# Moving columns of the projections' matrix products read in groups of 16, last group first

## The chip, the cores and the metric

The kernel runs on one NeuronCore of a Trainium2 chip. The metric is the device time of one execution in microseconds (us). Three runs of the kernel before gave 1861.96, 1864.28 and 1864.6 us; the median, 1864.28 us, is the time that the change is measured against.

## The reference, cut to what matters

Two layers of a hybrid block work on an activation of 512 positions by 1024 features. Each layer is a chain of matrix products with small element-wise pieces between them:

```python
h = rms_norm(x, g_pre_mix)
proj = h @ w_in                          # 1024 -> 6728 columns: q, k, v, qi, ki, wi, xr, gr, zu, zv, gates
y_a = dsa_attention(q, k, v, qi, ki, wi) # 8 heads, top-128 keys by an indexer
y_b = rg_lru(conv(xr)) * gelu(gr)
y_c = chunked_spatial_gating(gelu(zu), rms_norm(gelu(zv)), w_spatial, b_spatial)
branch = einsum('nbsw,nwd->nbsd', stack(y_a, y_b, y_c), w_branch)
merged = einsum('bsnd,nbsd->bsd', sigmoid(gates), branch)
x = x + rms_norm(merged @ w_out, g_post_mix)
f = square(relu(rms_norm(x, g_pre_ffn) @ w_ffn_up)) @ w_ffn_down   # 1024 -> 4096 -> 1024
x = x + rms_norm(f, g_post_ffn)
x = x + rms_norm((p_i @ w_ple) * sigmoid(x @ w_ple_gate), g_post_ple)
```

## The kernel before, in words

**Layout.** Activations lie transposed: features on the 128 partitions, the 512 positions along the free dimension, eight tiles of 128x512 for 1024 features. So most products take a 128x128 block of weights as the stationary operand and a 128x512 activation tile as the moving one, and sum eight such products (one for each tile of features) in one 2 KB bank of PSUM, 128 partitions by 512 columns of 4 bytes.

**Three products for one.** Each operand is held as a sum of a high and a low part of the type float32r (`split`, line 365, for activations; `prep`, line 231, for weights). A product of two such operands is three matmuls into the same bank: high by high, low weights by high activations, high weights by low activations. The helper `mm3` (line 296, its matmuls on lines 297, 298 and 299) issues these three; `gemm` (line 301) calls it for each tile of features.

**The callers.** `gemm` serves the input projections (`proj`, line 555), the branch products (`branch`, line 870), the output projection (line 1036), the feed-forward products (lines 1062 and 1071), the two products of the last stage (lines 1103 and 1122) and, in halves of 256 columns, the last three tiles of the output projection and of the last gate (`gemm_halves`, line 321). `mm3` is also called by itself for the spatial gating (line 765, moving operands of 256 columns) and for the gates of the recurrence (lines 829 and 830). `gemm_arriving` (line 334, matmul on line 355) starts the first outputs of a stage while their activation tiles are still being made, tile by tile, in whole tiles of 512 columns or in two halves of 256; `ordered` (line 311) writes the order of its instructions down by hand. `tokens` (line 578, matmul on line 589) computes the two projections whose result is wanted with positions on the partitions: there the activations are the stationary operand, and the weights, 512 columns wide, the moving one.

**What is not reached by the change.** The indexer's and the attention's products (lines 655, 658 and 941), the transposes (lines 162, 433, 630 and 927), the sums of squares (line 407) and the 120 small matmuls at the start (line 113) call the engine directly.

**What feeds and follows.** Weights arrive by SyncE's queue in 128x1024 blocks (line 236); ScalarE makes the high part (line 242) and VectorE the low part (line 243), three blocks ahead (`getw`, line 246). Eight banks of PSUM are used in turn; VectorE or ScalarE reads a bank once its last matmul is done. Waits between engines are put in by the framework from the tiles and regions that the instructions read and write; each engine works through its own instructions in the order of the program. Work of the indexer, attention and recurrence is dealt out between matmuls by a clock that counts estimated matmul time (`tick`, line 285).

Of the kernel before, what the change touches and what calls it, by code (L numbers as in the profile page):

```python
# [19 lines left out]
KT = 8  # L20
# [30 lines left out]
def hybrid_block_kernel(ctx, tc, xT, pT, pos, vec, bsp, freq, w_in, w_tok, w_lru, w_sp, w_br, w_out, w_up, w_dn, w_ple, w_gate, out, depth=DEPTH, dbg=None):  # L51
    nc = tc.nc
    V, A, G, PE = nc.vector, nc.scalar, nc.gpsimd, nc.tensor
# [13 lines left out]
    def tmp(dt=F32):  # L67
        return tp.tile([128, S], dt, tag="tmp", name=nm("tmp"), bufs=NTMP)
# [4 lines left out]
    def bank():  # L73
        return pp.tile([128, 512], F32, tag="ps", name=nm("ps"), bufs=8)

    def slot(tag, dt=F32, big=False):
        return cp.tile([128, 4, S] if big else [128, S], dt, tag=tag, name=nm(tag))
# [5 lines left out]
    def width(r):  # L83
        return r.stop - r.start
# [146 lines left out]
    def prep():  # L231
        i = nprep[0]
        nprep[0] += 1
        key, src = order[i]
        raw = wp.tile([128, 1024], F32, tag="wr", name=nm("wr"), bufs=3)
        nc.sync.dma_start(raw, src)
        if key[0] == "sp":
            r3 = raw.rearrange("p (g t) -> p g t", g=8)
            G.affine_select(out=r3, in_=r3, compare_op=ALU.is_ge, fill=0.0, base=0, pattern=[[0, 8], [1, 128]], channel_multiplier=-1)
        hi = wp.tile([128, 1024], F32R, tag="wh", name=nm("wh"), bufs=NWB)  # L240
        lo = wp.tile([128, 1024], F32R, tag="wl", name=nm("wl"), bufs=NWB)
        A.copy(hi, raw)  # L242
        V.tensor_sub(lo, raw, f32v(hi))  # L243
        prepared[key] = (hi, lo)

    def getw(key, ahead=LA):
        assert order[nget[0]][0] == key, (order[nget[0]][0], key)
        nget[0] += 1
        while nprep[0] < min(nget[0] + ahead, len(order)):
            prep()  # L250
        return prepared.pop(key)
# [33 lines left out]
    def tick(us):  # L285
        clk[0] += us
        run_later()
        run_tasks()
# [4 lines left out]
            tick(0.3)  # L293


    def mm3(ps, wh, wl, xh, xl, start, stop):
        PE.matmul(ps, wh, xh, start=start, stop=False)  # L297
        PE.matmul(ps, wl, xh, start=False, stop=False)  # L298
        PE.matmul(ps, wh, xl, start=False, stop=stop)  # L299

    def gemm(ps, w, xs, kk, c0=0, st=None, r=FULL):

        h3, l3 = [v.rearrange("p (k c) -> p k c", k=kk) for v in w]
        for k in range(kk):
            if st is not None and k == kk - 2:
                st.partial()
            mm3(ps, h3[:, k, c0:c0 + 128], l3[:, k, c0:c0 + 128], xs[k][0][:, r], xs[k][1][:, r], k == 0, k == kk - 1)
            tick(0.65 * width(r) / S)

    @contextmanager  # L310
    def ordered(last):

        cur = nc.cur_bb
        n0 = len(cur.bb.instructions)
        yield
        for i in cur.bb.instructions[n0:]:
            if i.engine in last:
                tc.add_manual_dep(i, last[i.engine], mybir.DependencyInfo(mybir.DependencyClass.NoSync, mybir.DependencyReason.DATA), reason="ordered")
            last[i.engine] = i.name
# [14 lines left out]
    def gemm_arriving(keys, xs, source, ranges, arrived=None, lag=LAG, tail=TAIL):  # L334


        n = len(keys)
        ws = [getw(key, 0) for key in keys[:-1]]
        pss = [bank() for _ in keys]
        last = {}  # L340
        for r in ranges:
            gen = source(r)
            for k in range(KT):
                with ordered(last):
                    next(gen)
                    todo = [(o, k) for o in range(len(ws))]
                    if len(ws) < n and k == lag:
                        ws.append(getw(keys[-1], 0))
                        todo += [(n - 1, q) for q in range(k + 1)]
                    if r is ranges[-1] and k >= KT - tail:  # L350
                        todo = [] if k < KT - 1 else [(o, q) for o in range(n) for q in range(KT - tail, KT)]
                    for i, (o, q) in enumerate(todo):
                        h3, l3 = [v.rearrange("p (k c) -> p k c", k=KT) for v in ws[o]]
                        for m in range(3):
                            PE.matmul(pss[o][:, r], (h3, l3, h3)[m][:, q], xs[q][m // 2][:, r], start=q == 0 and m == 0, stop=q == KT - 1 and m == 2)  # L355
                        if r is ranges[-1] and q == KT - 1 and o < n - 1:
                            prep()
                tick(0.65 * len(todo) * width(r) / S)
            if arrived is not None:
                arrived(r)  # L360
        while nprep[0] < nget[0] + LA:
            prep()
        return pss
# [84 lines left out]
    class Norm:  # L448
# [16 lines left out]
        def source(self, r):  # L465
            while r.start not in self.gens:
                tick(0.1)
            return self.gens[r.start]
# [48 lines left out]
    for k in range(KT):  # L517
        if k in FIRST:
            c = slice(128 * k, 128 * (FIRST + [KT])[FIRST.index(k) + 1])
# [12 lines left out]
    for l in range(depth):  # L532
# [22 lines left out]
        def proj(name, ahead=LA):  # L555
            ps = bank()
            gemm(ps, getw(("in", l, name), ahead), XS, KT)
            return ps
# [19 lines left out]
        def tokens(n, fn):  # L578


            ws = [[v.rearrange("p (k c) -> p k c", k=2) for v in getw(("tok", l, n, c), LA if c == 0 else 0)] for c in range(4)]
            for t0 in (0, 2):
                pss = [bank(), bank()]
                for k in range(KT):
                    wh, wl = [v[:, k % 2] for v in ws[k // 2]]
                    for t, ps in enumerate(pss, t0):
                        xh, xl = [v[:, t * 128:(t + 1) * 128] for v in XS[k]]
                        for i, (x, w) in enumerate(((xh, wh), (xl, wh), (xh, wl))):
                            PE.matmul(ps, x, w, start=k == 0 and i == 0, stop=k == KT - 1 and i == 2)  # L589
                        tick(0.65)  # L590
                    if t0 == 2 and k in (1, 3, 5):
                        prep()
                for t, ps in enumerate(pss, t0):
                    fn(t, ps)
# [7 lines left out]
        for j in range(4):  # L602
            ps = first[j]
# [7 lines left out]
            xh, xl = slot(f"B{j}", F32R), slot(f"B{4 + j}", F32R)  # L611
# [5 lines left out]
        ps = proj("ki")  # L617
# [28 lines left out]
        for j in range(4):  # L646
            ps = proj(f"qi{j}")
# [90 lines left out]
        for j in range(4):  # L738
            ps = proj(f"zu{j}")
# [16 lines left out]
        for j in range(4):  # L756
            mx = tmp()
            m3 = mx.rearrange("p (c t) -> p c t", c=4)
            fs = slice(j * 128, (j + 1) * 128)
            for hf in range(2):  # L760
                ps = bank()
                p3 = ps.rearrange("p (c t) -> p c t", c=2)
                for c in range(2):
                    cc = 2 * hf + c
                    mm3(p3[:, c], zvh[:, cc, fs], zvl[:, cc, fs], wsh[:, j], wsl[:, j], True, True)
                for s in range(2):
                    r = slice(64 * s, 64 * s + 64)
                    V.scalar_tensor_tensor(m3[r, 2 * hf:2 * hf + 2], p3[r, :, s * 128:(s + 1) * 128], vc[r, V_GV + j:V_GV + j + 1],
                                           bs3[r, j, None, :].to_broadcast([64, 2, 128]), op0=ALU.mult, op1=ALU.add)
            G.tensor_mul(mx, mx, gzu[:, j])  # L770
            MX.append(mx)
            tick(1.3)
            tick(1.3)
            if j % 2 == 1:
                gelu_gate(j // 2, LA if j == 3 else LA - 1)
# [47 lines left out]
        for j in range(4):  # L823
            if j == 2:

                th0 = gate(2, 0, ahead=LA - 1)
            xc, xh, xl = XC[j]
            pr, pi = bank(), bank()
            mm3(pr, w3[0][:, j], w3[1][:, j], xh, xl, True, True)
            mm3(pi, w3[0][:, 4 + j], w3[1][:, 4 + j], xh, xl, True, True)  # L830
            r, i = tmp(), tmp()
            A.activation(r, pr, AF.Sigmoid, bias=col(V_BA + j))
            A.activation(i, pi, AF.Sigmoid, bias=col(V_BX + j))
            G.tensor_mul(xc, xc, i)
            Rg.append(r)
            tick(1.3)
# [160 lines left out]
        for j in range(4):  # L997
            f = rope(proj(f"q{j}"))
            q2, ql = (slot(f"A{j}", F32R), slot(f"A{4 + j}", F32R)), tmp(F32R)
            for s in range(2):  # L1000
                r, other = slice(64 * s, 64 * s + 64), slice(64 - 64 * s, 128 - 64 * s)
# [15 lines left out]
        for d in range(8):  # L1017
            if d % 2 == 0:
                w = getw(("br", l, 0, d // 2))
# [14 lines left out]
        for d in range(5):  # L1034
            ps = bank()
# [8 lines left out]
        ps = bank()  # L1044
# [52 lines left out]
        for c in range(2):  # L1097
            w = getw(("ple", l, c), ahead=1)
            if c == 1:
                bc = st3.rstd_bc()  # L1100
            for i in range(4):
                ps = bank()
# [14 lines left out]
        for d in range(5):  # L1117
            if d < 4:
                ps = first[d]
            else:  # L1120
                ps = bank()
# [95 lines left out]
```

## Time and profile before

| | |
|---|---|
| median of three runs | 1864.28 us (1861.96 to 1864.6) |
| the profiled execution's own time | 1858.77 us |
| its span, first to last instruction | 1857.0 us |
| busy TensorE matmuls (PE) | 1812.3 us, 8798 matmuls |
| busy weight loads (PEld) | 1502.8 us, 8798 loads |
| busy VectorE (DVE) / ScalarE (ACT) / GpSimd (POOL) | 1158.3 / 801.9 / 365.0 us |
| mean granted clock of TensorE | 0.993 |
| moved from and to HBM | 164.19 and 2.10 MB, 90 GB/s over the span |

The profile is one execution. Matmuls overlap one another, and the ends that the profile gives them are modelled: a 512-column matmul has a row of 0.39 us while the next one starts 0.23 us after it. What a matmul costs in a dense stretch is therefore read from the starts of neighbours, and not from the duration of a row. Weight loads run beside matmuls and have rows of their own. [...]

### The profile page before, as it was taken

The numbers are of one execution on the slowest core, as the hardware profiler recorded it, in microseconds if no ns is written. First come the engines' busy times: TensorE is split into PE (matmuls) and PEld (weight loads), VectorE is DVE, ScalarE is ACT, GpSimd is POOL, SyncE is SP. The second block draws the span as 40 slices with busy tenths as digits, with TensorE's granted clock in tenths as the row PEclk, the third lists the DMA queues.
The fourth block names the chain that finished last, engine by engine and source line by source line (L and its number), as shares of the span: only waits on it lengthen the run. The fifth ranks groups of instructions, "written<-read, shape, count | busy, mean of one in ns | idle before, by whom it ended". The sixth has DMA issues, their size and how long they took to land.

```text
span 1857.0 us, 22869 instructions
## 1 busy us (share of the span) xinstructions
PE 1812.3 (98%) x8798; PEld 1502.8 (81%) x8798; DVE 1158.3 (62%) x1939; ACT 801.9 (43%) x1292; POOL 365.0 (20%) x292
## 2 busy tenths in 40 slices
PE   8999999999999999999999999999999999999997
PEld 7778777788888888888886887887888888888886
DVE  7689976666386253533686999666563852535355
ACT  5456436564453222223454572465544432222233
POOL 3513222210240000003454141222003200000033
PEclk9999999999999999999999999999999999999999
DMA  5122222222223322232212222222222223232321
GB/s 172 63 91 89 91 94 91 68 80 80 84 88 103 102 93 101 96 109 91 92 58 96 69 91 94 99 80 69 91 80 91 91 91 102 91 102 93 112 80 58
DMA packets 49679, 167.77 MB, mean 90 GB/s; under 512 B 6049, under 2 KB 8865, under 8 KB 49569
## 3 DMA queue, kind: packets, MB, share of 16 engines
q1 hardware_dynamic: 47376, 163.64, 26.5%
q10 hardware_dynamic: 2192, 2.67, 0.4%
q8 instruction: 69, 1.13, 0.3%
q14 instruction: 42, 0.34, 0.1%
HBM read 164.19 MB, written 2.10 MB: 90 GB/s over the span
## 4 chain that ended last, share of the span: by engine, by line
PE 73%; DVE 12%; POOL 6%; issue 4%; ACT 4%; DMA 0%; SPq 0%; POOLq 0%; ACTq 0%; DVEq 0%
PE ps L297 21%; PE ps L299 20%; PE ps L298 20%; PE ps L355 3%; PE ps L589 3%; DVE tmp L693 2%; DVE wl L243 2%; DVE m L691 2%; POOL tmp L574 1%; POOL tmp L575 1%; PE ps L941 1%; PE ps L658 1%; POOL sacc L397 1%; POOL X L482 1%; PE ps L655 1%
## 5 line engine op out<-in xcount | busy, mean ns | idle before, releaser
L242 ACT CAST wh<-wr 128x1024 fp32r<-128x1024 f32 x303 | 317.1, 1049 | 459.7 <-PE ps L299 381.4
L243 DVE TENSOR_TENSOR wl<-wr,wh 128x1024 fp32r<-128x1024 f32 x303 | 386.4, 1278 | 197.0 <-ACT wh L242 196.9
L297 PE MATMUL ps<-xh,wh 128*128 128x512 f32 (+1 forms) x1296 | 504.8, 389 | 0.0
L298 PE MATMUL ps<-xh,wl 128*128 128x512 f32 (+1 forms) x1296 | 495.0, 382 | 1.2 <-DVE wl L243 1.2
L299 PE MATMUL ps<-xl,wh 128*128 128x512 f32 (+1 forms) x1296 | 495.1, 382 | 0.0
L397 POOL TENSOR_TENSOR sacc<-sacc,tmp 128x256 f32<-128x256 f32 (+1 forms) x99 | 109.8, 1109 | 894.8 <-issue 584.5
L297 PEld LDWEIGHTS ps<-xh,wh 128*128 128x128 f32 x1296 | 243.7, 188 | 49.0 <-issue 4.9
L299 PEld LDWEIGHTS ps<-xl,wh 128*128 128x128 f32 x1296 | 243.7, 188 | 48.3
L298 PEld LDWEIGHTS ps<-xh,wl 128*128 128x128 f32 x1296 | 244.1, 188 | 44.4 <-DVE wl L243 2.0
L299 PE MATMUL ps<-V,wh 128*128 128x512 f32 (+1 forms) x528 | 195.4, 370 | 0.0
L297 PE MATMUL ps<-K,wh 128*128 128x512 f32 (+1 forms) x432 | 158.2, 366 | 0.0
L298 PE MATMUL ps<-K,wl 128*128 128x512 f32 (+1 forms) x432 | 157.8, 365 | 0.0
L299 PE MATMUL ps<-B,wh 128*128 128x512 f32 x336 | 130.9, 390 | 0.0
L297 PE MATMUL ps<-A,wh 128*128 128x512 f32 x320 | 125.0, 390 | 0.0
L298 PE MATMUL ps<-A,wl 128*128 128x512 f32 x320 | 124.5, 389 | 0.0
L1076 DVE TENSOR_TENSOR M<-M,ps 128x512 f32<-128x512 f32 x48 | 33.0, 688 | 141.4 <-PE ps L299 141.4
L299 PEld LDWEIGHTS ps<-V,wh 128*128 128x128 f32 x528 | 99.5, 188 | 16.8
L1064 DVE TENSOR_TENSOR tmp<-ps,R 128x512 f32<-128x512 f32 x64 | 43.8, 689 | 108.6 <-PE ps L299 108.6
L355 PE MATMUL ps<-xl,wh 128*128 128x256 f32 (+1 forms) x264 | 87.9, 333 | 7.8 <-DVE xl L502 7.1
L298 PEld LDWEIGHTS ps<-K,wl 128*128 128x128 f32 x432 | 81.5, 189 | 13.1
L297 PEld LDWEIGHTS ps<-K,wh 128*128 128x128 f32 x432 | 81.5, 189 | 13.1
L355 PE MATMUL ps<-xh,wh 128*128 128x256 f32 (+1 forms) x264 | 86.2, 327 | 1.2 <-ACT xh L492 1.2
(239 smaller groups left out, 2742.6 us busy)
## 6 DMA issues: line engine op xcount, KB each, us to landing
wr<-in_w_in_dram SPq DMA_DIRECT2D x95, 512.0 KB, 3.3
wr<-in_w_up_dram SPq DMA_DIRECT2D x64, 512.0 KB, 3.3
wr<-in_w_dn_dram SPq DMA_DIRECT2D x64, 512.0 KB, 3.3
wr<-in_w_br_dram SPq DMA_DIRECT2D x24, 512.0 KB, 3.2
wr<-in_w_tok_dram SPq DMA_DIRECT2D x16, 512.0 KB, 3.2
wr<-in_w_out_dram SPq DMA_DIRECT2D x16, 512.0 KB, 3.2
wr<-in_w_gate_dram SPq DMA_DIRECT2D x16, 512.0 KB, 3.2
X<-in_xT_dram SPq DMA_DIRECT2D x8, 256.0 KB, 5.7
```

Of the source, the lines that this page charges most:

```text
L242: A.copy(hi, raw)
L243: V.tensor_sub(lo, raw, f32v(hi))
L297: PE.matmul(ps, wh, xh, start=start, stop=False)
L298: PE.matmul(ps, wl, xh, start=False, stop=False)
L299: PE.matmul(ps, wh, xl, start=False, stop=stop)
L355: PE.matmul(pss[o][:, r], (h3, l3, h3)[m][:, q], xs[q][m // 2][:, r], start=q == 0 and m == 0, stop=q == KT - 1 and m == 2)
L397: G.tensor_add(sacc[:, r], sacc[:, r], self.q[r.start, r.stop])
L589: PE.matmul(ps, x, w, start=k == 0 and i == 0, stop=k == KT - 1 and i == 2)
L691: V.max(m8, (sc if r == 0 else wk)[:, :n])
L693: V.match_replace(wk[:, :n], m8, (sc if r == 0 else wk)[:, :n], -3.0e38)
L1064: V.tensor_mul(t, ps, R)
L1076: V.tensor_add(F[d], F[d], ps)
```

## The change

A helper `back` takes a view of a tile whose last dimension is a multiple of 16 columns, sees it as groups of 16, and runs over the groups from the last to the first; the columns of a group stay in ascending order. A helper `mm` issues a matmul whose moving operand and whose output are both seen through `back`, so every column's sum lands where it landed before. The stationary operand is left as it is. `mm3`, `gemm_arriving` and `tokens` issue their matmuls through `mm`. The number of instructions, their order, their operands and their tiles are the same.

```diff
+    def back(v):
+
+        return v.rearrange("p (b c) -> p b c", c=16)[:, ::-1]
+
+    def mm(ps, w, x, start, stop):
+
+        PE.matmul(back(ps), w, back(x), start=start, stop=stop)
+
     def mm3(ps, wh, wl, xh, xl, start, stop):
-        PE.matmul(ps, wh, xh, start=start, stop=False)
-        PE.matmul(ps, wl, xh, start=False, stop=False)
-        PE.matmul(ps, wh, xl, start=False, stop=stop)
+        mm(ps, wh, xh, start, False)
+        mm(ps, wl, xh, False, False)
+        mm(ps, wh, xl, False, stop)
@@ gemm_arriving
-                            PE.matmul(pss[o][:, r], (h3, l3, h3)[m][:, q], xs[q][m // 2][:, r], start=q == 0 and m == 0, stop=q == KT - 1 and m == 2)
+                            mm(pss[o][:, r], (h3, l3, h3)[m][:, q], xs[q][m // 2][:, r], q == 0 and m == 0, q == KT - 1 and m == 2)
@@ tokens
-                            PE.matmul(ps, x, w, start=k == 0 and i == 0, stop=k == KT - 1 and i == 2)
+                            mm(ps, x, w, k == 0 and i == 0, k == KT - 1 and i == 2)
```

## Rows read from the trace of the kernel before

**Rows 1.** The page: busy time by engine, and the chain that ended last, by engine.

```profile
PE 1812.3 (98%) x8798; PEld 1502.8 (81%) x8798; DVE 1158.3 (62%) x1939; ACT 801.9 (43%) x1292; POOL 365.0 (20%) x292
...
PE 73%; DVE 12%; POOL 6%; issue 4%; ACT 4%; DMA 0%; SPq 0%; POOLq 0%; ACTq 0%; DVEq 0%
```

**Rows 2.** One stretch of the feed-forward stage: columns as named in the first line.

```profile
core 0: us, PE busy (x) PEld busy (x) DVE busy (x) ACT busy (x) POOL busy (x), PEclk, DMA share, GB/s
...
600.00:750.00 150.00, 150.00 (x663) 124.24 (x662) 62.51 (x72) 40.82 (x48) 0.00 (x0) 1.00 0.28 95
```

**Rows 3.** Timeline of PE, feed-forward, 512 columns: start, duration; first and sixteenth matmul.

```profile
600.44 0.39 PE L297 MATMUL ps<-xh,wh 128*128 128x512 f32 x1
...
603.84 0.39 PE L297 MATMUL ps<-xh,wh 128*128 128x512 f32 x1
```

**Rows 4.** Timeline of PE in `gemm_arriving`, 256 columns: first and twenty-first matmul.

```profile
535.55 0.28 PE L355 MATMUL ps<-xh,wh 128*128 128x256 f32 x1
...
537.95 0.28 PE L355 MATMUL ps<-xl,wh 128*128 128x256 f32 x1
```

**Rows 5.** Whole span, one line's instructions alone: lines 297, 298, 299, 355, 589, in turn.

```profile
0.00:1857.00 1857.00, 867.25 (x2256) 424.44 (x2256) 0.99 0.27 90
...
0.00:1857.00 1857.00, 855.24 (x2256) 424.84 (x2256) 0.99 0.27 90
...
0.00:1857.00 1857.00, 855.43 (x2256) 424.35 (x2256) 0.99 0.27 90
...
0.00:1857.00 1857.00, 135.65 (x792) 117.31 (x792) 0.99 0.27 90
...
0.00:1857.00 1857.00, 96.92 (x384) 74.06 (x384) 0.99 0.27 90
```

**Rows 6.** Groups of PE by shape: 256-column matmuls of lines 297 and 355.

```profile
L355 PE MATMUL ps<-xh,wh 128*128 128x256 f32 x176 | 51.2, 291 | 0.0
...
L297 PE MATMUL ps<-xh,wh 128*128 128x256 f32 x96 | 27.5, 286 | 0.0
L297 PE MATMUL ps<-K,wh 128*128 128x256 f32 x96 | 27.5, 286 | 0.0
...
L297 PE MATMUL ps<-wh,K 128*128 128x256 f32 x32 | 9.0, 282 | 0.0
```

**Rows 7.** Timeline of PE in the first stage: first and sixth of six neighbours.

```profile
23.60 0.63 PE L355 MATMUL ps<-xh,wh 128*128 128x512 f32 x1
...
25.73 0.63 PE L355 MATMUL ps<-xl,wh 128*128 128x512 f32 x1
```

**Rows 8.** The stretch around them, columns as in Rows 2.

```profile
23.50:26.00 2.50, 2.50 (x7) 1.92 (x7) 2.39 (x8) 0.00 (x0) 0.00 (x0) 0.50 0.02 7
```

**Rows 9.** Lines 433 and 927: weight loads of one column repeated, and of 128 columns.

```profile
L433 PEld LDWEIGHTS ps<-ident,rt x40: 132/134/179, 38.1 to 1848.5; 128*128 128x128 f32 x40
...
L927 PEld LDWEIGHTS ps<-ident,tmp x160: 138/141/144, 291.8 to 1356.9; 128*128 128x128 f32 x160
```

**Rows 10.** Lines 372 and 481 on VectorE, min/median/max ns: four separate groups of 64 columns, one run of 256.

```profile
L372 DVE SCALAR_TENSOR_TENSOR V<-ps,rt,V x16: 467/476/484, 245.2 to 1176.6; 128x256 fp32r<-128x256 f32 x16
...
L481 DVE SCALAR_TENSOR_TENSOR B<-B,gp,ps x32: 468/472/480, 922.7 to 1853.0; 128x256 f32<-128x256 f32 x32
```

**Rows 11.** PE's waits for other engines: in total, times, longest us.

```profile
PE ps L355 <- DVE xl L502: 7.1, 9, 3.8
PE ps L655 <- DVE A L642: 6.7, 10, 1.2
PE ps L589 <- DVE wl L243: 5.0, 2, 2.5
```

## The prediction

> **What bounds the kernel now.** I read the page first: busy times, then the chain that ended last [rows 1]. Matmuls fill 1812.3 of 1857.0 us, so TensorE is without work for 44.7 us in all, and 73% of the chain is its own. A busy row of overlapping matmuls says little of their pace, so next I took a dense stretch [rows 2]: 150 us in the feed-forward stage without a gap, granted clock 1.00 (the 2.4 GHz level), VectorE and ScalarE busy for 62.5 and 40.8 us of it, the DMA engines for 0.28. Nothing but TensorE can set the time there. Then the pace, from neighbours' starts. Fifteen steps of 512-column matmuls take 3.40 us [rows 3], 226.7 ns each. Twenty steps of 256 columns take 2.40 us [rows 4], 120.0 ns each. The difference, 106.7 ns for 256 columns, is 0.417 ns a column, one column per clock at 2.4 GHz; what is left is the same in both, 13.3 to 13.4 ns per matmul. So a matmul costs its columns plus a fixed part, and there is no slack that would swallow a slower column: the moving read and the write of the sums run as fast as the array takes them.
>
> PE's waits for other engines are few [rows 11]; the longest total is 7.1 us. A slower TensorE could win back a part of the 44.7 us and no more.
>
> **The change, part by part.** No instruction is added, removed or moved. No queue is passed, no DMA touched, no buffer changed, no wait added by intention. What changes is the address pattern of two operands of 2256 matmuls on each of lines 297, 298 and 299, 792 on line 355 and 384 on line 589 [rows 5]: 7944 of 8798.
>
> - *How many are narrow.* On line 297, 96 + 96 + 32 = 224 have 256 columns, and lines 298 and 299 have as many; on line 355 it is 176 for each of three products [rows 6]. Together 3 x 224 + 3 x 176 = 1200. The other 6744 have 512 columns.
> - *What they cost now.* 6744 x 226.7 ns = 1528.9 us, 1200 x 120.0 ns = 144.0 us; 1672.9 us, 90% of the span. Any price on them is therefore paid nearly in full, since nothing stands beside them that ends later.
> - *How many jumps.* A 512-column operand is now 32 runs of 16 with 31 jumps back between them, a 256-column one 16 runs with 15. That makes 6744 x 31 + 1200 x 15 = 227,064 jumps, in reading and writing at once.
> - *Price of a jump.* No row shows a TensorE moving operand in pieces, so I bound it. Above: each matmul already begins with a jump, to another moving tile and back to the first column of the bank, together with the change of weights, and all that costs 13.4 ns. At that price the change adds 227,064 x 13.4 ns = 3043 us. Below: zero. A gain is excluded for the columns, which already come at one per clock. In the fixed part it could be 13.4 ns x 7944 = 106 us at the very most; no row gives a reason for it, since every matmul still starts with a jump of its own.
> - *Which end I take.* The nearest row is TensorE's other read. A weight load of one column repeated 128 times takes 134 ns, of 128 neighbouring columns 141 ns [rows 9]: a pattern that isn't a plain run costs that engine nothing. On VectorE an operation on 256 columns that reads one operand and writes its result in four separate groups of 64 takes 476 ns, a like one on plain runs 472 [rows 10]: 4 ns at most for three jumps in reading and three in writing. Finally the low clock: in the first stage, at a granted clock of 0.50 (1.2 GHz) [rows 8], five steps take 2.13 us [rows 7], 426 ns each, just 512 columns at that clock; the 13.4 ns vanish. What the start of a matmul needs is then hidden behind its neighbours' columns, which suggests that addresses are prepared ahead. I take zero per jump and zero per matmul.
> - *What follows a matmul.* The bank is read when the last product is done; in which order its columns were filled changes no wait. VectorE's and ScalarE's reads keep their pattern.
>
> Sum: 1858.8 us for the profiled execution (span 1857.0 and 1.8 us around it), plus 0. The median of the runs shown is 1864.3, 5.5 us or 0.3% above that execution; I forecast for the median, **1864.3 us**, and expect the runs' own spread, 1862 to 1865, around it.
>
> [...]
>
> **The rivals.**
>
> 1. *A jump costs one column's time.* Place: inside each changed matmul, 31 or 15 times. Price: 0.417 ns x 227,064 = 94.6 us, 1959 us. For it: columns run at the clock, so a single clock lost at a run's end has nowhere to hide. Against it: rows 9 and the vanishing start cost of rows 7. It decides once a jump costs 0.017 ns on average (3.8 us in all), that is, nearly at once; it could also be more than one clock.
> 2. *A longer pattern costs a fixed sum per matmul*, in reading or unpacking the instruction. At a quarter of the present 13.4 ns it gives 3.35 ns x 7944 = 26.6 us, 1891 us; doubled, 106 us, 1971 us. Against it: there is a whole matmul of 227 ns in which to prepare the next.
> 3. *Broken-up columns go at half rate*, as if the clock were at its lower level: 6744 x (426.7 - 226.7) ns + 1200 x (213.3 - 120.0) ns = 1349 + 112 = 1461 us, 3325 us. For it there is no row; rows 9 speak against it.
> 4. *Order kept for more than before.* If the framework takes a backward view of a half tile for more than it covers, writers of one half wait for matmuls on the other. Only line 355's three stages of two halves have such views: 72, 96 and 96 narrow matmuls a half, 8.6 + 11.5 + 11.5 = 31.7 us at most, 1896 us. Rows 11 already show that line's wait, 7.1 us, which would grow.
> 5. *The change does nothing.* Moving operand and sums are permuted alike, so a compiler could straighten both. The time is then that of the forecast.
> 6. *Faster by more than noise*: a part of the fixed 13.4 ns goes. 0.5 ns per matmul would be 4 us, 1860 us.
>
> **How the numbers follow.** About 0.2% of the time, 3.7 us, is what a measurement of this kernel can tell from no change; spread over 7944 matmuls this is 0.47 ns each, hardly more than one clock. Forecast with rival 5: 0.63. Rival 1: 0.13, of which 0.08 at one clock or less. Rival 2: 0.08. Rival 3: 0.08. Rival 4: 0.03. Rival 6: 0.05. Slower is 1 to 4, 0.32. The likeliest case alone would have 1858 to 1868. The range has to take in rivals 1, 2 and 4 as far as one clock per jump: up to 1960 it holds 0.63 + 0.08 + 0.06 + 0.03 = 0.80; below it begins at 1858, the profiled execution's own time.
>
> **What the profile after would show.** If I am right: fifteen steps in the feed-forward stage still take 3.40 us and twenty narrow ones 2.40 us, with a busy count of about 663 in any dense 150 us there. Rival 1: 239.6 and 126.2 ns per step, so both grow, by 31 and 15 clocks. Rival 2: both grow by the same number of ns. Rival 3: 427 and 213 ns, at a granted clock of still 1.00. Rival 4: the pace is unchanged, and waits stand before line 355 or before ScalarE's line 492. The forecast is wrong if a dense step differs from 226.7 ns by over half a nanosecond.

## The result, and the profile after

The changed kernel took 1888.05 us (median of four runs, 1886.89 to 1888.52) against 1863.12 us before (four runs, 1861.19 to 1864.6): a ratio of 1.0137, with an interval of 1.0124 to 1.015. That is 24.9 us more. The profiled execution of after has a span of 1885.2 us, 28.2 us above the 1857.0 of before.

The page of after, busy time by engine and the chain that ended last, to be read against [rows 1]:

```profile
PE 1846.2 (98%) x8798; PEld 1500.9 (80%) x8798; DVE 1157.6 (61%) x1939; ACT 801.7 (43%) x1292; POOL 363.2 (19%) x292
...
PE 80%; DVE 8%; POOL 5%; issue 3%; ACT 3%; DMA 0%; SPq 0%; POOLq 0%; DVEq 0%; ACTq 0%
```

All the counts are the same. VectorE, ScalarE and GpSimd do the same work in the same time; only PE's busy time has grown, by 33.9 us, and with it PE's share of the chain, from 73% to 80%. PE's time without work fell from 44.7 to 1885.2 - 1846.2 = 39.0 us.

The same 150 us of the feed-forward stage as in [rows 2], with the same columns (PE, PEld, DVE, ACT, POOL busy and counts, granted clock as a share of full speed, DMA share, GB/s):

```profile
600.00:750.00 150.00, 150.00 (x645) 120.90 (x644) 58.68 (x67) 38.14 (x46) 0.00 (x0) 1.00 0.28 95
```

There are 645 matmuls where there were 663, without a gap and at the same granted clock of 1.00. The pace itself, from the timeline of PE in after (start us, duration): first a wide pair, 21 steps apart, then the first of 93 narrow matmuls in a row and the small one that ends them.

```profile
620.64 0.40 PE L302 MATMUL ps<-K,wh 128*128 128x512 f32 x1
...
625.54 0.40 PE L302 MATMUL ps<-K,wh 128*128 128x512 f32 x1
...
497.26 0.28 PE L302 MATMUL ps<-K,wh 128*128 128x256 f32 x1
...
508.21 0.28 PE L415 MATMUL ps<-ones,sacc 128*128 128x2 f32 x2
```

A wide step takes 4.90 / 21 = 233.3 ns, 6.7 ns more than the 226.7 of [rows 3]. A narrow one takes 10.95 / 93 = 117.7 ns, 2.3 ns **less** than the 120.0 of [rows 4]. (All matmuls of the change now have line 302, that of the helper.)

The chain of waits of after, start and length of its two longest pieces, shows where the time is paid:

```profile
548.70 329.00 PE ps L302 x1410
...
1481.59 329.00 PE ps L302 x1410
```

These are the feed-forward products of the two layers, 1410 wide matmuls each at 329.00 / 1410 = 233.3 ns. At the pace before they would take 319.6 us. So 2 x 9.4 = 18.8 us of the 28.2 are paid there, and the rest in stages where other work interrupts the stream.

### The profile page after: what moved, and what is told of

It reads as the page before. It is cut to its first block, busy times and chain, and to the rows that moved or that the text cites. A ratio compares the mean times of both kernels' runs of the same rounds, so it can differ in the third digit from the quotient of the medians.

```text
span 1885.2 us, 22932 instructions
## 1 busy us (share of the span) xinstructions
PE 1846.2 (98%) x8798; PEld 1500.9 (80%) x8798; DVE 1157.6 (61%) x1939; ACT 801.7 (43%) x1292; POOL 363.2 (19%) x292
## 4 chain that ended last, share of the span: by engine, by line
PE 80%; DVE 8%; POOL 5%; issue 3%; ACT 3%; DMA 0%; SPq 0%; POOLq 0%; DVEq 0%; ACTq 0%
PE ps L302 76%; PE ps L949 1%; PE ps L666 1%; PE ps L663 1%; DVE wl L243 1%; POOL sacc L405 1%; DVE tmp L701 1%; POOL X L490 1%; DVE m L699 1%; POOL tmp L583 1%; PE ps L935 1%; POOL tmp L582 1%; POOL B L863 1%; DVE M L618 1%; POOL tmp L866 1%
## 5 line engine op out<-in xcount | busy, mean ns | idle before, releaser
L302 PE MATMUL ps<-xh,wh 128*128 128x512 f32 (+1 forms) x1560 | 598.8, 384 | 1.0 <-ACT xh L500 1.0
L302 PE MATMUL ps<-xl,wh 128*128 128x512 f32 (+1 forms) x1560 | 590.8, 379 | 6.6 <-DVE xl L510 5.9
L302 PE MATMUL ps<-xh,wl 128*128 128x512 f32 (+1 forms) x1560 | 588.3, 377 | 0.0
L302 PEld LDWEIGHTS ps<-xl,wh 128*128 128x128 f32 x1560 | 293.3, 188 | 69.4 <-DVE xl L510 11.0
L302 PEld LDWEIGHTS ps<-xh,wh 128*128 128x128 f32 x1560 | 293.5, 188 | 60.8 <-issue 4.8
L302 PEld LDWEIGHTS ps<-xh,wl 128*128 128x128 f32 x1560 | 293.7, 188 | 52.4
L302 PE MATMUL ps<-V,wh 128*128 128x512 f32 (+1 forms) x624 | 224.6, 380 | 0.0
L302 PE MATMUL ps<-B,wh 128*128 128x512 f32 x416 | 158.6, 401 | 0.0
L302 PEld LDWEIGHTS ps<-B,wh 128*128 128x128 f32 x416 | 78.3, 188 | 19.1 <-issue 0.9
L302 PEld LDWEIGHTS ps<-A,wh 128*128 128x128 f32 x384 | 72.1, 188 | 17.8 <-ACT A L376 0.5
```

The source lines that it names most:

```text
L302: PE.matmul(back(ps), w, back(x), start=start, stop=stop)
```

## The experiments

All runs are of one core; where no ratio is given, a kernel ran once beside the kernel before, whose own runs in those sessions lay between 1858.07 and 1864.38 us. A total within 3 us of it says nothing; the pace of neighbours in the trace says more.

### Which side pays: reading or writing

```diff
-        PE.matmul(back(ps), w, back(x), start=start, stop=stop)
+        PE.matmul(ps, w, back(x), start=start, stop=stop)      # read16
+        PE.matmul(back(ps), w, x, start=start, stop=stop)      # write16
```

Expected of `read16`:

> Only the moving operand is read backward in groups of 16; the sums are written straight, so the groups of columns of every product stand in reversed order in the result. After the change a 512-column step takes 233.3 ns (226.7 before), a 256-column step 117.7 ns (120.0 before). If the price lies in reading: 233.3 and 117.7 ns again, about 1887 us. If it lies in writing the sums: 226.7 and 120.0 ns, about 1863 us. If each side has a share, between the two.

Expected of `write16`:

> Only the sums are written backward in groups of 16; the moving operand is read straight, so here too the groups of columns stand in reversed order in the result. If the price lies in writing: 233.3 and 117.7 ns, about 1887 us. If in reading: 226.7 and 120.0 ns, about 1863 us.

Measured: `read16` 1890.62 us, `write16` 1859.41 us, before 1859.15 us. The 150 us of the feed-forward stage, PE alone (busy and count, granted clock, DMA share, GB/s), in `read16`:

```profile
600.00:750.00 150.00, 150.00 (x644) 1.00 0.27 95
```

and its timeline, the first of 93 narrow matmuls and the small one behind them:

```profile
499.92 0.28 PE L302 MATMUL ps<-K,wh 128*128 128x256 f32 x1
...
510.87 0.28 PE L415 MATMUL ps<-ones,sacc 128*128 128x2 f32 x2
```

The same two views of `write16`:

```profile
600.00:750.00 150.00, 150.00 (x664) 1.00 0.27 96
```

```profile
494.33 0.28 PE L302 MATMUL ps<-K,wh 128*128 128x256 f32 x1
...
505.49 0.28 PE L415 MATMUL ps<-ones,sacc 128*128 128x2 f32 x2
```

Reading alone gives everything: 644 matmuls where after has 645, and narrow steps of 10.95 / 93 = 117.7 ns, as in after, so the little gain of the narrow ones comes from reading too. Writing alone is the kernel before: 664 matmuls, narrow steps of 11.16 / 93 = 120.0 ns. The address pattern of the sums costs nothing here when they are written in backward groups of 16 columns (1859.41 us against 1859.15).

### How long the pieces are

```diff
-        return v.rearrange("p (b c) -> p b c", c=16)[:, ::-1]
+        return v.rearrange("p (b c) -> p b c", c=C)[:, ::-1]   # C = 64, 256, 32, 8, 4, 1
```

Expected of groups of 64 and 256:

> Groups of 64 instead of 16, read and written backward: 7 jumps in a 512-column matmul instead of 31, 3 instead of 15 in a narrow one. Theory A (each jump has its price, and the start cost of 13.3 ns is nearly gone from a broken pattern: 20.0 ns over the columns with 31 jumps and 11.0 with 15 give 0.56 ns per jump and 2.6 ns per matmul): 213.3 + 2.6 + 7 x 0.56 = 219.8 ns and 106.7 + 2.6 + 3 x 0.56 = 111.0 ns, some 45 + 11 us under the kernel before, about 1807 us. Theory B (a broken pattern makes every column a little slower, 0.452 instead of 0.417 ns, whatever the groups): 233.3 and 117.7 ns, about 1887 us. Theory C (a jump has its price and the start cost stays): 226.7 + 7 x 0.2 = 228.2 ns, about 1869 us.

> Groups of 256: a 512-column matmul takes its two halves in reversed order, one jump; a narrow one is a plain run again. Theory A: 213.3 + 2.6 + 0.56 = 216.5 ns, and 120.0 ns for the narrow ones: 10.2 ns x 6744 = 69 us under the kernel before, about 1795 us. Theory B: 233.3 ns, about 1890 us. Theory C: 226.9 ns, about 1864 us.

Measured: 1860.99 and 1863.92 us, both within the spread of the kernel before. The same stretch, PE alone, of `groups64`:

```profile
600.00:750.00 150.00, 150.00 (x664) 1.00 0.28 98
```

and of `groups256`:

```profile
600.00:750.00 150.00, 150.00 (x663) 1.00 0.28 98
```

None of the three theories foresaw this. Seven breaks, or one, cost nothing at all, and gain nothing. Theory A fell (no gain), and theory B (every column of a broken pattern slower), and for theory C 7 breaks should have shown 1.5 ns a step, or 659 matmuls.

So I formed theory D (two limits, of which the slower counts) and tried shorter pieces.

> Groups of 32, read and written backward. Theory D (two limits, of which the slower one counts: the columns with the start cost of 13.3 ns, 226.7 and 120.0 ns; and the reading of the groups, each its columns at 0.417 ns and 0.625 ns more, so that 32 groups of 16 take 32 x 7.29 = 233.3 ns): 16 x 13.96 = 223.3 ns lies below 226.7, so 226.7 and 120.0 ns, about 1862 us. Theory E (broken patterns have no start cost at all, and groups of 64 were long enough to count as plain): 223.3 and 111.7 ns, 23 + 10 us faster, about 1830 us.

> Groups of 8. Theory D: 64 x (3.33 + 0.625) = 253.3 ns and 126.7 ns; 180 + 8 us over the kernel before, about 2048 us. Theory F (moving columns are fetched in pieces of fixed length, 16 columns or more, and a broken-off piece costs as much as a whole one): 64 x 7.29 = 466.7 ns and 233.3 ns, about 3615 us.

> Groups of 4. Theory D: 128 x (1.67 + 0.625) = 293.3 ns and 146.7 ns, about 2340 us. Theory F with pieces of 16: 128 x 7.29 = 933 ns and 467 ns, about 7040 us; with pieces of 8, a fourth of this above what groups of 8 gave per group.

Measured: groups of 32, 1886.24 us (four runs), a ratio of 1.0143 with an interval of 1.0125 to 1.0161; of 8, 1894.19 us; of 4, 1891.27 us. The stretch in `groups32`:

```profile
600.00:750.00 150.00, 150.00 (x645) 1.00 0.27 95
```

in `groups8`:

```profile
600.00:750.00 150.00, 150.00 (x645) 1.00 0.28 95
```

with the timeline around its narrow matmuls (a wide one, one step of 0.23 us ahead of 93 narrow steps, and the small one behind them):

```profile
501.36 0.40 PE L302 MATMUL ps<-V,wh 128*128 128x512 f32 x1
...
512.75 0.28 PE L415 MATMUL ps<-ones,sacc 128*128 128x2 f32 x2
```

and in `groups4`:

```profile
600.00:750.00 150.00, 150.00 (x645) 1.00 0.27 95
```

The count is 645 for 15, 31, 63 and 127 breaks in a matmul. **A break has no price.** Theory D (fell at 32, where it wanted 226.7 ns, and at 8 and 4, where it wanted 253 and 293) and theory F (467 ns and more) are both out. What counts in this stretch is only whether the pieces are short: at 32 columns and below a wide step takes 233.3 ns, at 64 and above 226.7. Groups of 32 are a little cheaper elsewhere. The chain of waits of `groups32` has the feed-forward products of the two layers as

```profile
548.45 329.00 PE ps L302 x1410
...
1481.40 327.66 PE ps L302 x1410
```

which is 233.3 ns a step in the first layer, as in after, but 232.4 in the second. The narrow gain is not so steady either: in groups of 8 the 93 narrow steps take 512.75 - 501.36 - 0.23 = 11.16 us, 120.0 ns, as before; the traces of groups of 32 and of 4 have 118.7 and 118.3 ns in the same place.

### Which direction, and one column at a time

```diff
-        return v.rearrange("p (b c) -> p b c", c=16)[:, ::-1]
+        return v.rearrange("p (b two c) -> p two b c", two=2, c=16)   # forward16; c=64: forward64
```

> Groups of 16 in ascending order, first the even groups and then the odd ones, read and written: as many breaks as in the change, but every one forward (except one). If the break itself costs: 233.3 and 117.7 ns, about 1887 us. If going backward costs: 226.7 and 120.0 ns, about 1862 us.

Measured: 1928.98 us, more than either branch. The stretch in `forward16`:

```profile
600.00:750.00 150.00, 150.00 (x627) 1.00 0.26 92
```

and two wide matmuls of its timeline, 15 steps apart:

```profile
599.67 0.41 PE L302 MATMUL ps<-xh,wh 128*128 128x512 f32 x1
...
603.27 0.40 PE L302 MATMUL ps<-xh,wh 128*128 128x512 f32 x1
```

A step takes 3.60 / 15 = 240.0 ns, another 6.7 ns more. So going backward is not what costs: this ascending order with breaks (even groups, then odd ones; no other was tried) is dearer still. Theory G came out of this: only the length of the ascending pieces counts.

> Groups of one column: the moving operand is read, and the sums are written, column by column from the last to the first, in one run with a step of -1. Theory G (what counts is whether the pieces that lie in ascending order are shorter than 64 columns; how many there are counts for nothing, since groups of 4, 8, 16 and 32 all took 233 ns): 233.3 and 117.7 ns, about 1889 us. Theory H (what counts is that the pattern is broken; a constant step is no break): 226.7 and 120.0 ns, about 1860 us. If every two neighbours have to be read in order: half rate, 427 and 213 ns, about 3325 us.

> Groups of 64, first the even ones and then the odd ones, each in order. In groups of 16 this order took 240 ns on the mean against 233.3 backward. Theory G: pieces of 64 cost nothing whatever their order: 226.7 and 120.0 ns, about 1860 us. If skipping forward has a price of its own: above 226.7 ns; by the 6.6 ns more that 31 forward breaks took, some 1.5 ns for 7, about 1870 us.

Measured: `groups1` 1889.92 us and `forward64` 1863.81 us. The stretch in `groups1`:

```profile
600.00:750.00 150.00, 150.00 (x644) 1.00 0.26 93
```

and in `forward64`:

```profile
600.00:750.00 150.00, 150.00 (x663) 1.00 0.29 98
```

Both as theory G has it. One run of 512 columns with a step of -1 pays what 128 pieces of 4 pay; pieces of 64 are free in this order too. Theory H (a constant step is no break) is out. Theory G leaves the extra 6.7 ns of `forward16` unexplained, so the order of short pieces counts for something as well.

### One product of three

```diff
     def mm3(ps, wh, wl, xh, xl, start, stop):
         mm(ps, wh, xh, start, False)
-        mm(ps, wl, xh, False, False)
-        mm(ps, wh, xl, False, stop)
+        PE.matmul(ps, wl, xh, start=False, stop=False)
+        PE.matmul(ps, wh, xl, start=False, stop=stop)
```

and likewise in the two other callers.

> Of the three products of every triple only the first (high by high) is read and written backward in groups of 16; the other two are as before. If the price belongs to the broken matmul alone: steps of 233.3, 226.7 and 226.7 ns, a third of the loss, about 1868 us. If it belongs to the neighbourhood (what runs beside a matmul, such as the next weight load, or the change from one pattern to the other): all three steps move, or the sum of three differs from 686.7 ns.

Measured: 1886.26 us, nearly the whole loss for a third of the matmuls. Timeline of PE in `first16`, the broken product of a triple each time: two that lie 35 triples apart in the first layer's feed-forward stage, and two that lie 36 apart in the second layer's output projection.

```profile
609.95 0.40 PE L302 MATMUL ps<-xh,wh 128*128 128x512 f32 x1
...
634.45 0.40 PE L302 MATMUL ps<-K,wh 128*128 128x512 f32 x1
...
1403.05 0.40 PE L302 MATMUL ps<-K,wh 128*128 128x512 f32 x1
...
1427.77 0.40 PE L302 MATMUL ps<-K,wh 128*128 128x512 f32 x1
```

Triples take 24.50 / 35 = 700.0 ns in the first stretch and 24.72 / 36 = 686.7 ns in the second, with the same instructions. The second is the sum of one broken and two plain steps. The first is three broken ones: the plain neighbours are as slow. Both branches of the expectation hold, each in its place, and a place keeps its pace from one interruption of the stream to the next.

### The narrow matmuls alone

```diff
-        return v.rearrange("p (b c) -> p b c", c=16)[:, ::-1]
+        return v.rearrange("p (b c) -> p b c", c=16)[:, ::-1] if v.shape[-1] == 256 else v
```

> Only the 1200 matmuls of 256 columns go backward in groups of 16, the 6744 wide ones are as before. Wide steps 226.7 ns, narrow ones 117.7 ns instead of 120.0: 1200 x 2.3 ns = 2.8 us less, 0.15%, which is at the edge of what can be measured; about 1858 to 1860 us beside 1861. If the narrow ones are faster only because wide ones stand elsewhere: 120.0 ns and no difference.

Measured: 1858.92 us (11 runs) against 1860.59 us (15 runs), a ratio of 0.9989 with an interval of 0.998 to 0.9998. The wide stretch in `narrow16`:

```profile
600.00:750.00 150.00, 150.00 (x663) 1.00 0.27 96
```

and its timeline around the narrow ones (again the wide one just ahead, one step of 0.23 us, then 93 narrow steps):

```profile
493.05 0.39 PE L302 MATMUL ps<-V,wh 128*128 128x512 f32 x1
...
504.23 0.28 PE L415 MATMUL ps<-ones,sacc 128*128 128x2 f32 x2
```

Wide as before, narrow (11.18 - 0.23) / 93 = 117.7 ns. This version is ahead of both kernels, by about 0.1%, with an interval that ends just short of no difference.

## Why the prediction was right or wrong

The forecast, no change, was wrong, also by the prediction's own sign: a dense step differs from 226.7 ns by 6.7, not by under half a nanosecond. The measured time lies in the range only because rivals 1 and 2, other mechanisms than the one found, had drawn it up to 1960 us; that is luck. By its steps:

- *What bounds the kernel*: right. Nothing but TensorE set the time, and nothing else changed.
- *Any price is paid nearly in full*: too strong. 6744 x 6.67 ns - 1200 x 2.3 ns = 42.2 us, and the spans differ by 28.2. PE's time without work took up 5.7 us, as the prediction allowed. The mean granted clock was 0.993 before and 0.995 after, which at these spans is worth 3 to 4 us; the prediction had no term for that. The rest has its place in the count of wide matmuls: I took all 6744 at 226.7 ns, and some were slower already. The timeline of the kernel before, just behind four small matmuls (first and eleventh of eleven neighbours):

```profile
542.59 0.40 PE L298 MATMUL ps<-xh,wl 128*128 128x512 f32 x1
...
544.90 0.39 PE L299 MATMUL ps<-xl,wh 128*128 128x512 f32 x1
```

and the same eleven of the kernel after:

```profile
545.75 0.40 PE L302 MATMUL ps<-xh,wl 128*128 128x512 f32 x1
...
548.09 0.40 PE L302 MATMUL ps<-xl,wh 128*128 128x512 f32 x1
```

  Before, ten steps take 2.31 us, 231 ns each: behind this interruption the stream doesn't come to 226.7 at once (behind the two transposes that follow, the trace has it there after three steps). After, ten steps take 2.34 us, 233 to 234 ns, about the pace of the long stretches. So a step here loses 2 to 3 ns, and one in the long feed-forward stretches 6.7. Counted over the starts of all matmuls in the two traces, the steps of under 260 ns from one wide matmul to the next (longer ones mostly hold a wait, an interruption or a granted clock of 0.50) number 6375 before, 227.3 ns on the mean, and 6394 after, 233.35 ns. That is 6375 x 6.06 ns = 38.6 us, where the sum above has 45.0. Less 2 us that the narrow ones gained, 5.7 and about 3.5, 27.4 us are left of it, close to the 28.2 measured.
- *Price of a jump, "which end I take"*: this is the step that failed. Zero per jump was right to the letter, from 15 jumps to 127 of them; zero **per matmul** was not: a wide matmul in short pieces costs 6.7 ns more. The rows that I drew on could not tell. [Rows 9] are the weight load, another reading than that of the moving columns; [rows 10] are another engine, with pieces of 64, a length that turned out free for TensorE too; and that the start cost vanishes at the low clock (426 ns for 512 columns at a granted clock of 0.50 [rows 7, rows 8]) did not mean that reading has room to spare at the high one. (No view gives a clock in GHz. The prediction's 2.4 and 1.2 GHz stand on the pace, 256 columns in 106.7 ns at a granted clock of 1.00 and 512 in 426 at 0.50; that a column costs just one clock is taken, not shown.) What took its place is a price for reading, paid as soon as the pieces are short and hardly more for more of them: `read16` pays it in full (644 matmuls per 150 us) and `write16` not at all (664). In places the plain neighbours pay it too (`first16`, 700.0 ns a triple against 686.7). What the kernel before did show, and I did not weigh, is that the pace of a plain stream is not one number (231 and 226.7 ns).
- *A gain in the fixed part has no reason*: the narrow matmuls did gain, 2.3 ns each (rival 6, in small). I had no row for it and still have no reason.
- *Rival 1* (a clock per jump) is excluded by the groups of 4, 8 and 32. *Rival 2* came nearest in time, 1891 us at a quarter of the start cost. Its place was wrong: the pattern costs nothing in writing and nothing in groups of 64, with an instruction of the same form (nor in `forward64`, whose moving operand has a dimension more in the trace), so it isn't unpacking; and its mark, both widths growing alike, failed. *Rival 3* (half rate) is out: 233.3 ns a step where it wanted 427. *Rival 4* is out: the longest total of waits of ScalarE's line 492 (500 in after) went from 21.1 to 20.9 us, and PE's waits for the line that ends a tile fell. In after (waits in total, times, longest, against 7.1 us in [rows 11]):

```profile
PE ps L302 <- DVE xl L510: 5.9, 9, 2.5
```

- *Rival 5* (a compiler straightens both sides) is out too, and with it the doubt whether pieces of 64 were read as pieces at all: the operand records in the traces have the moving operand of a wide matmul as 32 groups of 16 columns in after and as 8 groups of 64 in `groups64`, and as one run of 512 in before and `write16`.
- *The sums written in pieces*: `write16`, with the sums in 32 pieces, kept 664 matmuls per 150 us and 120.0 ns for narrow ones. `groups1` reads and writes column by column backward, not at half rate, and pays no more than groups of 16 do for reading alone (644 matmuls per 150 us in both); it doesn't exclude a price of writing that is hidden behind that of reading.

**What stays open.** That the price lies in reading short pieces of the moving operand is shown, and that it doesn't grow with their number (15 to 127 breaks). What in the reading makes the price isn't. Nor is why the border lies between 32 and 64 columns, why groups of 32 are a little cheaper in the second layer, why short pieces in even-then-odd order cost twice as much (240.0 ns a step against 233.3, where plain ones take 226.7), and why plain neighbours of a broken matmul are slow in one stretch and not in another. Groups between 32 and 64 weren't tried, nor other types of operand, nor a pace without a weight load for each matmul.

## What to carry to other kernels

Where a kernel is bound by wide float32r matmuls, a moving operand could here be read in pieces of 64 columns or more, backward or even-then-odd, for nothing; short backward pieces cost about 3% of a 512-column step at once, and from 32 columns down to one it hardly mattered how short they were. The sums could here be written in backward pieces of 16 for free (1859.41 us against 1859.15), so a permutation is better tried on the writing side first. And a matmul's price is read from the starts of its neighbours in the stage that matters, near interruptions and far from them: 42 us by one pace for all of them, with no allowance for waits and clock, stood against a loss of 28.

## What the runs showed of the hardware that was not expected

Many of the paces fit one small unit, on the mean over neighbours. 226.7, 233.3 and 240.0 ns are 34, 35 and 36 times 6.67 ns, the time of 16 columns at the 0.417 ns a column of [rows 3] and [rows 4]; 120.0 ns is 18 times that, and three narrow steps of 117.7 to 117.8 ns are 353 ns, 53 times. Plain, a wide matmul takes two of these units beyond its 32; in short backward pieces it takes three, in even-then-odd pieces of 16 four. Single steps do not: in `forward16` they alternate between about 236 and 244 ns. Nor does every mean: 232.4 ns in the second layer of `groups32` lies between two units. And with one broken matmul in three, a stretch settles at 686.7 or at 700.0 ns per triple and keeps to it, 103 or 105 units. What the unit is, no run shows.
